# One scratch layout for the values of a neighbourhood attention: written column by column, without a second copy

## The chip, the cores and the metric

The kernel runs on one core of one Trainium2 chip, as one launch. The metric is the device time of that launch in microseconds (us). A core has five engines with an instruction queue each: TensorE (PE, with its weight loads shown apart as PEld), VectorE (DVE), ScalarE (ACT), GpSimd (POOL) and SyncE (SP). SP, ACT and POOL also issue DMA transfers, which sixteen DMA engines carry out. Each queue is worked off in order; between engines, semaphores order the work.

## The reference

One layer of a bidirectional encoder is computed for two sequences, a prompt of 1024 tokens and a sample of 512, with the same weights; model width 1024, head size 64, all in float32. Two token mixers work side by side: branch A is attention of 8 query heads over 2 key/value heads, branch B is attention over a neighbourhood of 8 rows × 16 columns on a grid that is 64 tokens wide (token t has row t // 64 and column t % 64).

```python
z = xn @ w_in            # q_A | k_A | v_A | q_B | k_B | v_B | gate_A | gate_B
o_a = _gqa_attention(qa, ka, va)
o_b = _neighbourhood_attention(qb, kb, vb, rpb)
merged = sigmoid(ga) * (o_a @ w_proj_a) + sigmoid(gb) * (o_b @ w_proj_b)
h = h + merged @ w_out
h = h + square(relu(rmsnorm(h) @ w_mlp_up)) @ w_mlp_down
```

A last RMSNorm follows. What matters here is v_B: 8 heads of 64 values for each token, projected token by token and later read as strips of the grid.

## The kernel before

Float32 products are made of three matmuls on a high and a low part of each operand (`mm3`); a value of branch B is therefore kept as 128 numbers, its 64 high parts and 64 low parts.

The kernel runs `run` for the sample first (called trunk 0 here, NB = 1, names with `s0`), then for the prompt (trunk 1, NB = 2, names with `s1`), and then one MLP for both. In `run`, two rounds g = 0 and 1 follow each other, one for each half of the heads. A round has a projection stage and an attention stage of branch A:

- Projection stage (pool `phR`). `load_a` and `load_v` load the weights by SP into raw buffers (`rawp`, three of them) and split them into high and low parts (L199 on ACT, L206 on DVE). For each tile `tt` of 128 tokens, that is two rows of the grid, PE makes `z`; `values(tt - 2)` makes the values of branch B for four heads into `zv` and splits them into `vt` (L648 on ACT, L649 on DVE), a tile of 128 tokens × 4 heads × 128 numbers with two buffers; ACT issues its store to the scratch `vd` in DRAM (L652), one tile late, through `pending` and `flush`. `heads_t` transposes queries and keys, and ACT copies them to `kT` and `qT` (L626, L628). At a stage's end the values and heads of the last two tiles come close together, with some matmuls of a gate (`fill.pull`) between.
- Attention stage (pool `phA`). `s_tile` makes a tile of scores into one of two PSUM buffers (`big`, L772 and L773), DVE takes the maximum, ACT the exponential into a tile `p` (L778), POOL scales it (L781); PE transposes `p` and multiplies it by the values of branch A (`pv`). Between them stand matmuls of the gate of branch A (`gate`, `fill`), whose results ACT stores to `zg` (L435). `phA` reuses the SBUF memory of `phR`; a tile of the one waits for the last access, a DMA's too, to the tile of the other that lay there.

In trunk 1 the attention stage also issues, on SP, two copies per unit (L808), 16 per round, 32 in all, from DRAM to DRAM: from the scratch `vd`, whose rows are tokens, to four scratches `vst[j]`, one for each strip of 32 columns, in the order that branch B reads.

Branch B follows (pool `phB`). `prep_v(h, j)` loads a strip of the values of head h: in trunk 1 with one load from `vst[j]` (L950), in trunk 0 with four loads from `vd`, one for each row a of four (L956 to L958). `v_unit` multiplies by it. Then come `phG`, which merges the branches, and the MLP.

The order of instructions on every engine is set by a planner of the framework, which goes by the order of the program, by the readiness of operands and buffers and by costs of its own; some instructions are held in program order by hand. The stores of ACT and the loads of SP share eight DMA semaphores, and a transfer can wait for the one before it on the same semaphore, whichever queue that was on.

Of the kernel before, what the change touches and what calls it, by code (L numbers as in the profile page):

```python
# [11 lines left out]
F32 = mybir.dt.float32  # L12
# [6 lines left out]
P = 128  # L19
# [3 lines left out]
GRID_W = 64  # L23
# [38 lines left out]
def encoder(ctx: ExitStack, tc: tile.TileContext, xs, outs, w):  # L62
    nc = tc.nc
    dram = ctx.enter_context(tc.tile_pool(name="dram", bufs=1, space=bass.MemoryType.DRAM))
# [28 lines left out]
    def mm(name):  # L93
        return pmm.tile([P, 512], F32, tag="mm", name=name)
# [175 lines left out]
    def flush():  # L270
        while pending:
            pending.pop(0)()
# [117 lines left out]
    class Trunk:  # L390
# [22 lines left out]
        def xh(self, tb, c):  # L413
            return self.xhl[tb][0][c // 4][:, c % 4, :]
# [4 lines left out]
    def run(tr, nxt, first):  # L419
        N, x, T, NT, NB = tr.N, tr.x, tr.T, tr.NT, tr.NB  # L420
        xh, xl = tr.xh, tr.xl
        rows = T // GRID_W
        halves = rows // 8

        vd = dram.tile([T, 8, P], F32, name=f"vd{N}")
        vst = [dram.tile([rows // 4, 32, 4, 8, P], F32, name=f"vst{N}_{j}") for j in range(4)] if NB == 2 else None
        zg = [dram.tile([D, T], F32, name=f"zg{N}_{i}") for i in range(2)]
        oad = dram.tile([4 * P, T], F32, name=f"oad{N}")
        obd = dram.tile([4 * P, T], F32, name=f"obd{N}")
# [99 lines left out]
        for g in range(2):  # L529
            with phase(f"phR{N}_{g}") as ph:  # L530
# [107 lines left out]
                def values(tt):  # L638

                    tb, j = divmod(tt, 4)  # L640
                    nm = f"{N}_{g}_{tt}"
                    js = slice(j * P, (j + 1) * P)
                    zv = mm(f"zv{nm}")[:, :256]
                    for k in range(NC8):
                        mm3(zv, xh(tb, k)[:, js], xl(tb, k)[:, js], wv[k][0], wv[k][1], k == 0, k == NC8 - 1)
                    vt = pre.pop("vt", None) or ph.tile([P, 4, P], F32R, tag="vt", name=f"vt{nm}", bufs=2)
                    zv4 = zv.rearrange("p (h d) -> p h d", d=HD)
                    nc.scalar.activation(vt[:, :, 0:HD], zv4, AF.Copy)  # L648
                    nc.vector.tensor_tensor(vt[:, :, HD:P], zv4, vt[:, :, 0:HD].bitcast(F32), op=ALU.subtract)  # L649
                    flush()  # L650
                    pending.append(
                        lambda: nc.scalar.dma_start(vd[tt * P : (tt + 1) * P, 4 * g : 4 * g + 4, :], vt.bitcast(F32))  # L652
                    )

                def chain(tt, z, rt):
# [34 lines left out]
                for tt in range(NT):  # L690
                    tb, j = divmod(tt, 4)
# [68 lines left out]
            with phase(f"phA{N}_{g}") as ph:  # L760
                units = [(h, qb) for h in range(4) for qb in range(NB)]
                PP = {}

                def s_tile(u, j):
                    h, qb = u
                    nm = f"{N}_{g}_{h}_{qb}_{j}"
                    q0 = (qb * 4 + j) * P
                    lhs = qT[h % 2][:, h // 2, q0 : q0 + P]
                    s = big(f"s{nm}")[:, :T]
                    for kb in range(NB):  # L770
                        ks = slice(kb * 512, kb * 512 + 512)
                        nc.tensor.matmul(s[:, ks], lhs, kT[:, 0, ks], start=True, stop=False)  # L772
                        nc.tensor.matmul(s[:, ks], lhs, kT[:, 1, ks], start=False, stop=True)  # L773
                    nm_ = sml.tile([P, 1], F32, tag="nm", name=f"nm{nm}")
                    nc.vector.tensor_reduce(nm_, s, axis=AX.X, op=ALU.max, negate=True)  # L775
                    p = ph.tile([P, T], F32, tag="P", name=f"p{nm}", bufs=8)
                    l = sml.tile([P, 1], F32, tag="l", name=f"l{nm}")
                    nc.scalar.activation(p, s, AF.Exp, bias=nm_, accum_out=l)  # L778
                    rl = sml.tile([P, 1], F32, tag="rl", name=f"rl{nm}")
                    nc.vector.reciprocal(rl, l)  # L780
                    nc.gpsimd.tensor_scalar(p, p, rl, 1.0, op0=ALU.mult, op1=ALU.mult)  # L781
                    PP[u, j] = p

                o_of = {}

                def pv(u, kc, hi, lo):
                    h, qb = u
                    if kc == 0:
                        o_of[u] = mm(f"o{N}_{g}_{h}_{qb}")
                    o = o_of[u]  # L790
                    nc.tensor.matmul(o, vhl[:, kc, :], hi, start=(kc == 0), stop=False)
                    nc.tensor.matmul(o, vhl[:, kc, :], lo, start=False, stop=(kc == NT - 1))
                    if kc == NT - 1:
                        r0 = (g * 4 + h) * HD
                        finish_o(o, 512, oad[r0 : r0 + HD, qb * 512 : qb * 512 + 512], ph, f"A{N}_{g}_{h}_{qb}")

                for j in range(4):
                    s_tile(units[0], j)
                    fill.pull(2)
                queue = []  # L800
                LAG = 2
                for ui, u in enumerate(units):
                    h, qb = u
                    if NB == 2:
                        hs = slice(4 * g, 4 * g + 4)
                        for a in range(2 * (ui % 2), 2 * (ui % 2) + 2):
                            c0 = (0, 8, 24, 32)[ui // 2]
                            nc.sync.dma_start(  # L808
                                vst[ui // 2][:, :, a, hs, :].rearrange("k c h d -> k c (h d)"),
                                vd[:, hs, :].rearrange("(k a c) h d -> a k c (h d)", a=4, c=GRID_W)[a, :, c0 : c0 + 32],  # L810
                            )
                    if first:
                        bias_row(g * 4 + ui)
                        if g == 0 and ui == 1:
                            early["a"] = load_a(1)
                        if g == 0 and ui == 2:
                            early["v"] = load_v(1, slot)
                    nxt_u = units[ui + 1] if ui + 1 < len(units) else None
                    sdone = 0
                    for kc in range(NT):  # L820
                        pt = mm(f"pT{N}_{g}_{h}_{qb}_{kc}")
                        for j in range(4):
                            nc.tensor.transpose(  # L823
                                pt[:, j * P : (j + 1) * P], PP[u, j][:, kc * P : (kc + 1) * P], ident
                            )
                        hi = ph.tile([P, 512], F32R, tag="pth", name=f"pth{N}_{g}_{h}_{qb}_{kc}", bufs=3)
                        lo = ph.tile([P, 512], F32R, tag="ptl", name=f"ptl{N}_{g}_{h}_{qb}_{kc}", bufs=3)
                        nc.scalar.activation(hi, pt, AF.Copy)  # L828
                        nc.vector.tensor_tensor(lo, pt, hi.bitcast(F32), op=ALU.subtract)  # L829
                        queue.append((u, kc, hi, lo))  # L830
                        if nxt_u is not None:
                            while sdone < 4 and kc >= ((0, 1, 3, 4) if NB == 2 else (0, 0, 1, 2))[sdone]:
                                s_tile(nxt_u, sdone)
                                sdone += 1

                        fill.pull(1 if NB == 1 or kc % 4 < 3 else 0)
                        if len(queue) > LAG:
                            pv(*queue.pop(0))
                fill.drain()
                for item in queue:  # L840
                    pv(*item)
# [80 lines left out]
        with phase(f"phB{N}") as ph:  # L922
# [22 lines left out]
            def prep_v(h, j):  # L945
                if h not in strips:
                    strips[h] = slot([P, 4, rows // 4, P], F32R, f"vs{N}_{h}")
                v = strips[h]
                if NB == 2:
                    nc.sync.dma_start(  # L950
                        v[:, j, :, :].bitcast(F32), vst[j][:, :, :, h, :].rearrange("k c a d -> (c a) k d")
                    )
                    return
                c0 = (0, 8, 24, 32)[j]
                for a in range(4):
                    nc.sync.dma_start(  # L956
                        v[a * 32 : a * 32 + 32, j, :, :].bitcast(F32),
                        vd[:, h, :].rearrange("(k a c) d -> a c k d", a=4, c=GRID_W)[a, c0 : c0 + 32],  # L958
                    )

            def load_qk(pr, hold=None):
# [229 lines left out]
            for i in range(n + 4 - NB):  # L1191
                if moved:
                    slot_no[0] = i
                if i < n - 8:
                    f = (5 if i < 2 else 2 + i % 2) if NB == 1 else 5 - (i % 6 == 5)
                else:
                    f = 3 + i % 2 if NB == 1 else 8
# [3 lines left out]
                if i < n:  # L1201
# [4 lines left out]
                    h, j = units[i]  # L1206
# [57 lines left out]
        with phase(f"phG{N}") as ph:  # L1264
# [65 lines left out]
            for half in range(2):  # L1330
                wo = wos[half]
                hc = slice(half * 512, half * 512 + 512)
                for tt in range(NT):
                    tb, j = divmod(tt, 4)
# [53 lines left out]
                    if half == 1:  # L1388
# [12 lines left out]
                        else:  # L1401
# [10 lines left out]
                            if 3 <= tt <= 5:  # L1412
                                j = tt - 3
# [563 lines left out]
```

## Time and profile before

| what | before |
|---|---|
| median of 3 runs | 2136.41 us (2136.06 to 2136.95) |
| the profiled execution | 2136.87 us, of which the span from first to last instruction is 2135.0 us |
| granted TensorE clock, mean | 0.997 of full speed |
| copies `vst <- vd` (L808) | 32 of 256 KB, on SP, issued from 452.2 to 791.2 us |
| stores `vd <- vt` (L652) | 24 of 256 KB, on ACT, issued from 35.1 to 652.7 us |
| strip loads `vs <- vst` (L950) | 32 of 256 KB, on SP |
| strip loads `vs <- vd` (L956) | 128 of 32 KB, on SP |

The page of the profile gives busy time by engine, the span in 40 slices with the granted clock and the DMA engines' mean busy share, the DMA queues, and the costliest groups of instructions. Further views are a list of waits (who waited for whom, total, times, longest), a timeline (start, duration, engine, line, operation, tiles; in brackets the idle time before it and what ended it; neighbours of one kind are merged, "x6"), and windows (for a stretch of time: its length, then the busy time and the count of instructions of PE, PEld, DVE, ACT and POOL, the granted clock, the share of the DMA engines and GB/s). A small q behind an engine's name (SPq, ACTq) is its queue of DMA issues; the duration there is that of issuing, not of the transfer. L212 and L206 are helpers that many stages use, so tiles tell stages apart: `zvs` is the value projection, `ss` the scores of branch A, `gpss` a gate.

### The profile page before, as it was taken

The page shows a single profiled execution, that of the slowest core. Times are in us where ns is not written, and L with a number is a line of the kernel's source. Part 1 is how long each engine was busy: PE and PEld are TensorE (multiplying, and loading weights), DVE is VectorE, ACT ScalarE, POOL GpSimd, SP SyncE. Part 2 cuts the span into 40 slices and gives each one's busy share as a digit, 9 for nine tenths or more (in the row PEclk, how much of TensorE's full clock was granted, in tenths as well). Part 3 has the DMA queues.
Part 4 walks back from the last instruction along what each step waited for, and adds up shares of the span by engine and source line. Part 5 has one row for each costly group of instructions (what it writes and reads, how often), then busy time and mean ns, then how long its engine had stood idle before and what let it go on. Part 6 is the DMA issues. An engine that isn't in the chain of part 4 may idle for free.

```text
span 2135.0 us, 31762 instructions
## 1 busy us (share of the span) xinstructions
PE 2099.9 (98%) x10871; PEld 1840.2 (86%) x10871; DVE 1483.2 (69%) x2793; ACT 1146.3 (54%) x2487; POOL 362.0 (17%) x446
## 2 busy tenths in 40 slices
PE   9999999999989999999999999999999999999998
PEld 8888778988888888888888899999999988888887
DVE  6665786767647756787882877778777777759563
ACT  6664653767556645555531556556655643434352
POOL 2232310323233314442101200003000000000000
PEclk9999999999999999999999999999999999999999
DMA  6437557520133038876472666578445799688561
GB/s 192 133 99 212 148 165 254 184 89 29 59 111 107 25 97 245 244 219 196 153 246 103 203 196 193 162 249 210 158 146 158 259 351 344 215 276 282 166 203 64
DMA packets 340072, 381.31 MB, mean 179 GB/s; under 512 B 30911, under 2 KB 267079, under 8 KB 339911
## 3 DMA queue, kind: packets, MB, share of 16 engines
q1 hardware_dynamic: 301687, 313.99, 46.9%
q10 hardware_dynamic: 31072, 45.11, 6.0%
q0 software_dynamic: 7152, 20.19, 3.5%
q8 instruction: 86, 1.41, 0.3%
q14 instruction: 75, 0.61, 0.1%
HBM read 282.68 MB, written 105.71 MB: 182 GB/s over the span
## 4 chain that ended last, share of the span: by engine, by line
PE 53%; DVE 1%; issue 0%; ACT 0%; POOLq 0%; POOL 0%; ACTq 0%; DVEq 0%
PE dn L212 20%; PE ua L212 6%; PE ud L212 6%; PE uc L212 6%; PE ops L212 4%; PE ub L212 3%; PE ppbs L212 2%; PE ppas L212 2%; PE dnf L212 2%; PE pt L353 0%; PE obs L212 0%; PE gpss L212 0%; PE sbs L212 0%; PE ptbs L1126 0%; DVE A L1452 0%
## 5 line engine op out<-in xcount | busy, mean ns | idle before, releaser
L212 PE MATMUL dn<-wd,ah 128*128 128x512 f32 x1248 | 384.3, 389 | 0.0
L212 PEld LDWEIGHTS dn<-wd,ah 128*128 128x128 f32 x1248 | 234.2, 188 | 48.7
L212 PE MATMUL dn<-wd,al 128*128 128x512 f32 x624 | 242.8, 389 | 0.0
L1451 ACT ACTIVATE ah<-ar 128x512 fp32r<-128x512 f32 x168 | 104.4, 628 | 206.0 <-PE dn L212 186.7
L212 PE MATMUL gpss<-xs_0h,w_gs 128*128 128x512 f32 x512 | 188.7, 402 | 0.8 <-DVE ot_Bs L472 0.4
L1452 DVE TENSOR_TENSOR al<-ar,ah 128x512 fp32r<-128x512 f32 x168 | 114.4, 687 | 75.5 <-ACT ah L1451 67.9
L212 PE MATMUL ud<-B,A 128*128 128x384 f32 x768 | 143.6, 334 | 0.7 <-DVE c L1569 0.7
L212 PE MATMUL uc<-B,A 128*128 128x384 f32 x768 | 143.7, 334 | 0.0
L212 PE MATMUL ua<-B,A 128*128 128x384 f32 x768 | 138.8, 334 | 0.0
L212 PEld LDWEIGHTS dn<-wd,al 128*128 128x128 f32 x624 | 117.1, 188 | 24.2
L781 POOL TENSOR_SCALAR ps<-ps,rls 128x1024 f32<-128x1024 f32 (+1 forms) x96 | 96.8, 1010 | 226.4 <-DVE rls L780 201.0
L212 PEld LDWEIGHTS ud<-B,A 128*128 128x128 f32 x768 | 133.9, 188 | 1.1 <-DVE c L1569 1.1
L212 PEld LDWEIGHTS uc<-B,A 128*128 128x128 f32 x768 | 134.1, 188 | 0.2 <-ACT A L1451 0.2
L212 PEld LDWEIGHTS ua<-B,A 128*128 128x128 f32 x768 | 133.7, 188 | 0.2
L829 DVE TENSOR_TENSOR ptls<-pTs,pths 128x512 fp32r<-128x512 f32 x160 | 107.7, 686 | 37.3 <-ACT pths L828 36.3
L828 ACT ACTIVATE pths<-pTs 128x512 fp32r<-128x512 f32 x160 | 94.0, 597 | 73.4 <-PE pTs L823 71.3
L212 PE MATMUL ops<-wh_os,mgs 128*128 128x512 f32 x384 | 119.4, 390 | 0.0
L775 DVE TENSOR_REDUCE nms<-ss 128x1 f32<-128x1024 f32 (+1 forms) x96 | 99.9, 1041 | 25.6 <-PE ss L773 25.1
L212 PEld LDWEIGHTS gpss<-xs_0h,w_gs 128*128 128x128 f32 x512 | 96.3, 189 | 18.9 <-DVE w_gs L206 0.7
L778 ACT ACTIVATE ps<-ss,nms 128x1024 f32<-128x1024 f32 (+1 forms) x96 | 93.2, 972 | 23.4 <-DVE nms L775 20.6
L180 POOL TENSOR_TENSOR rs_f<-ms_f,mhalf 128x1 f32<-128x1 f32 x6 | 4.0, 667 | 590.7 <-DVE ms_f L176 590.7
L823 PEld LDWEIGHTS pTs<-ident,ps 128*128 128x128 f32 x640 | 77.7, 140 | 28.6 <-POOL ps L781 4.3
(287 smaller groups left out, 5152.4 us busy)
## 6 DMA issues: line engine op xcount, KB each, us to landing
ar<-ud SPq DMA_DIRECT2D x120, 512.0 KB
br<-in_w_mlp_down_dram SPq DMA_DIRECT2D x72, 512.0 KB
rawu<-in_w_mlp_up_dram SPq DMA_DIRECT2D x64, 512.0 KB
ud<-c ACTq DMA_DIRECT2D x128, 192.0 KB
raw_gs<-in_w_in_dram SPq DMA_DIRECT2D x32, 512.0 KB
ud<-cs SPq DMA_DIRECT2D x64, 192.0 KB
tbs<-pbs SPq DMA_DIRECT2D x24, 384.0 KB
bhs<-tbs SPq DMA_DIRECT2D x24, 384.0 KB
```

The source lines that it names most:

```text
L180: nc.gpsimd.tensor_tensor(r[:, :n], m[:, :n], mhalf[:, :n], op=ALU.pow)
L212: op = nc.tensor.matmul(out, a, b, **kw)
L775: nc.vector.tensor_reduce(nm_, s, axis=AX.X, op=ALU.max, negate=True)
L778: nc.scalar.activation(p, s, AF.Exp, bias=nm_, accum_out=l)
L781: nc.gpsimd.tensor_scalar(p, p, rl, 1.0, op0=ALU.mult, op1=ALU.mult)
L823: nc.tensor.transpose(pt[:, j * P : (j + 1) * P], PP[u, j][:, kc * P : (kc + 1) * P], ident)
L828: nc.scalar.activation(hi, pt, AF.Copy)
L829: nc.vector.tensor_tensor(lo, pt, hi.bitcast(F32), op=ALU.subtract)
L1451: nc.scalar.activation(hi, src, AF.Copy)
L1452: nc.vector.tensor_tensor(lo, src, hi.bitcast(F32), op=ALU.subtract)
```

## The change

The scratch `vd` gets a layout of its own: group of four rows, column, row in the group, head, numbers. The four scratches `vst` and the copies into them go. The store of a value tile writes its two rows of 64 tokens side by side into each column, so its destination counts 2 rows × 64 columns × 2 KB, where its source still counts 128 partitions × 2 KB. A strip of trunk 1 is loaded from `vd` itself, with one load; the loads of trunk 0 read the same bytes from the new places. What is computed stays the same.

```diff
-        vd = dram.tile([T, 8, P], F32, name=f"vd{N}")
-        vst = [dram.tile([rows // 4, 32, 4, 8, P], F32, name=f"vst{N}_{j}") for j in range(4)] if NB == 2 else None
+        vd = dram.tile([rows // 4, GRID_W, 4, 8, P], F32, name=f"vd{N}")
...
                     flush()
+                    to = vd[tt // 2, :, tt % 2 * 2 : tt % 2 * 2 + 2, 4 * g : 4 * g + 4, :]
                     pending.append(
-                        lambda: nc.scalar.dma_start(vd[tt * P : (tt + 1) * P, 4 * g : 4 * g + 4, :], vt.bitcast(F32))
+                        lambda: nc.scalar.dma_start(
+                            to.rearrange("c r h d -> r c (h d)"), vt.bitcast(F32).rearrange("p h d -> p (h d)")
+                        )
                     )
...
-                    if NB == 2:
-                        hs = slice(4 * g, 4 * g + 4)
-                        for a in range(2 * (ui % 2), 2 * (ui % 2) + 2):
-                            c0 = (0, 8, 24, 32)[ui // 2]
-                            nc.sync.dma_start(
-                                vst[ui // 2][:, :, a, hs, :].rearrange("k c h d -> k c (h d)"),
-                                vd[:, hs, :].rearrange("(k a c) h d -> a k c (h d)", a=4, c=GRID_W)[a, :, c0 : c0 + 32],
-                            )
...
+                c0 = (0, 8, 24, 32)[j]
                 if NB == 2:
                     nc.sync.dma_start(
-                        v[:, j, :, :].bitcast(F32), vst[j][:, :, :, h, :].rearrange("k c a d -> (c a) k d")
+                        v[:, j, :, :].bitcast(F32), vd[:, c0 : c0 + 32, :, h, :].rearrange("k c a d -> (c a) k d")
                     )
                     return
-                c0 = (0, 8, 24, 32)[j]
                 for a in range(4):
                     nc.sync.dma_start(
                         v[a * 32 : a * 32 + 32, j, :, :].bitcast(F32),
-                        vd[:, h, :].rearrange("(k a c) d -> a c k d", a=4, c=GRID_W)[a, c0 : c0 + 32],
+                        vd[:, c0 : c0 + 32, a, h, :].rearrange("k c d -> c k d"),
                     )
```

## The prediction

> **What bounds the kernel now.** I read the page's span and busy rows first, then PE's own waits, then the timeline around the longest of them. "Trunk 0" is the sample (512 tokens, first), "trunk 1" the prompt (1024).
>
> ```profile
> span 2135.0 us, 31762 instructions
> PE 2099.9 (98%) x10871; PEld 1840.2 (86%) x10871; DVE 1483.2 (69%) x2793; ACT 1146.3 (54%) x2487; POOL 362.0 (17%) x446
> PE zvs L212 <- ACT wh_vs L199: 5.7, 1, 5.7
> PE sbs L212 <- DVE kBs L1015: 2.3, 2, 1.8
> ```
>
> TensorE is the bound: it idles about 35 us of 2135. So nothing is won by lighter transfers as such; a change counts only where PE waits, or comes to wait. PE's longest wait by far is a single one of 5.7 us on L199, the split of the value weights (`load_v`). Its chain, from the timelines of SP, ACT and PE:
>
> ```profile
> 538.33 0.41 DVE L206 TENSOR_TENSOR wgls<-rawkvs,wghs 128x256 fp32r<-128x256 f32 x1
> 574.53 12.34 SPq L808 DMA_DIRECT2D vsts<-vds  x6
> 586.99 4.00 SPq L245 DMA_DIRECT2D raw_vs<-in_w_in_dram  x2
> 598.32 1.06 ACT L199 ACTIVATE wh_vs<-raw_vs 128x1024 fp32r<-128x1024 f32 x1 [3.29 <-DMA raw_vs<-in_w_in_dram]
> 599.43 0.58 PE L212 MATMUL zvs<-wh_vs,xs_0h 128*128 128x256 f32 x1 [5.74 <-ACT wh_vs L199]
> 599.40:605.60 6.20, 5.59 (x24) 5.00 (x24) 0.00 (x0) 0.00 (x0) 0.53 0.27 77
> 436.70:439.66 2.96, 2.88 (x25) 2.69 (x23) 0.00 (x0) 0.00 (x0) 1.00 0.26 94
> ```
>
> SP issues in order. Six of the copies that the change removes (L808) stand ahead of the two loads of the value weights of trunk 1's second half; these go out at 586.99, share the engines with copies still moving, and PE stands until 599.43. The last two rows are windows of tile zvs alone: its 24 matmuls then take about 6.2 us at a granted clock of 0.53, where 25 took 2.96 us at 1.00, so 24 take 2.8 to 2.9. The stall costs 5.74 plus 6.17 − 2.88 = 3.29: **9.0 us** in all.
>
> **The change, part by part.** *Removed:* 32 copies `vst <- vd`.
>
> ```profile
> L808 SPq DMA_DIRECT2D vsts<-vds x32: 579/580/1127, 452.2 to 791.2; - x32
> L652 ACTq DMA_DIRECT2D vds<-vts x24: 326/326/368, 35.1 to 652.7; - x24
> SPq L808 <- DMA oads<-os_As: 29.7, 5, 9.3
> ```
>
> SP loses 32 issues of 0.58 us and the waits before them (the third row is the one that holds the last ones). The raw buffers that the load fills come free long before 587 (the last split that reads one ends at 538.7, first row of the chain above), so the load goes out early, or, if the planner leaves it at 587, meets empty queues: 1 MB at the 317 GB/s of the write below is 3.3 us, with the start and a split of 1.06 some 6, hence before 593.7, where PE came to stand. Either way the stall goes: −9.0. What is late next there is nothing that I see; bounds 0 and −9.0, and I take −9.0, the measured stall. Behind the 16 copies of trunk 1's second half (up to 791) the one longer wait in PE's list, sbs with 1.8, comes 190 us later; 0.
>
> *Reads (L950, L958):* as many pieces of 512 B, at other strides. They go out a head or several units ahead of the matmuls that use them, and none of PE's waits names them: 0, and without that cover a load's few us, once.
>
> *Writes (L652):* this is where the price is. The tile's 128 rows of 2 KB used to go to 128 evenly spaced rows. Now row and column swap: the destination is 2 × 64 pieces, outermost count 2. Windows in which only one such transfer moves show what an outermost count does:
>
> ```profile
> 437.52 0.33 ACTq L652 DMA_DIRECT2D vds<-vts  x1
> 438.36:439.18 0.82, 0.82 (x9) 0.82 (x8) 0.27 (x1) 0.82 (x3) 0.00 (x0) 1.00 0.84 317
> 531.05:534.55 3.50, 3.50 (x21) 2.97 (x20) 3.36 (x6) 2.72 (x5) 1.12 (x1) 1.00 0.23 74
> 562.42:565.74 3.32, 3.32 (x21) 2.75 (x20) 2.43 (x5) 2.50 (x6) 1.13 (x1) 1.00 0.24 78
> ```
>
> Both move 256 KB (0.82 us at 317 GB/s; 3.50 at 74). The write, 128 rows on both sides, has 0.84 of the 16 DMA engines busy; the copy, whose source is 4 × 32 rows, 0.23 to 0.24, four engines. I read this as: the outermost count is what gets spread. An outermost 2 then leaves two engines. Work per transfer: 0.82 × 0.84 × 16 = 11.0 engine-us for the write, 3.50 × 0.23 × 16 = 12.9 for the copy; on two engines **5.5 to 6.4 us** in place of 0.8. I take 5.5, its own row. It starts about 1.0 us after issue (437.52 to 438.36, rounded up).
>
> [...]
>
> Mid-stage this is hidden: `vt` has two buffers, and a write has about a tile's period to land (7 us, 437.52 to 444.42, two neighbouring writes). At the four ends of the projection stages the last tiles crowd, and I follow the last three writes A, B, C. The last tile's `vt` (L648, on ACT, ahead of the kT copies) needs A; then the exponentials L778 put their results where the pool before held `vt`, and need B and C. Trunk 1, first half, then second:
>
> ```profile
> 444.42 0.33 ACTq L652 DMA_DIRECT2D vds<-vts  x1
> 449.27 0.33 ACTq L652 DMA_DIRECT2D vds<-vts  x1
> 449.69 0.38 ACT L648 ACTIVATE vts<-zvs 128x256 fp32r<-128x256 f32 x1
> 451.27 0.33 ACTq L652 DMA_DIRECT2D vds<-vts  x1
> 455.86 1.12 ACT L778 ACTIVATE ps<-ss,nms 128x1024 f32<-128x1024 f32 x1 [0.48 <-DVE nms L775]
> 457.33 0.39 PE L772 MATMUL ss<-kTs,qTs 128*128 128x512 f32 x1
> 645.65 0.34 ACTq L652 DMA_DIRECT2D vds<-vts  x1
> 651.79 0.39 ACT L648 ACTIVATE vts<-zvs 128x256 fp32r<-128x256 f32 x1 [1.05 <-DMA vds<-vts]
> 658.26 1.12 ACT L778 ACTIVATE ps<-ss,nms 128x1024 f32<-128x1024 f32 x1
> 660.45 0.39 PE L772 MATMUL ss<-kTs,qTs 128*128 128x512 f32 x1
> ```
>
> First half: A moves 445.4 to 450.9, so the last `vt` starts 1.2 late and C is issued at 452.5. B ends at 456.4, C at 461.9. The exponential waits from 455.86 to 461.9, +6.0. PE's third score tile needs the score bank that it frees (at 455.86 + 1.12 = 456.98) and started at 457.33, 0.35 later: PE stands 5.7 us. At 6.4 us a write: A 451.8, B 458.2, C 464.6, stall 8.4. Behind the exponential ACT's whole queue stands, and PE's own order is fixed, so the gate matmuls behind that score tile can't fill in.
>
> Second half, same steps: the row at 651.79 shows that this wait exists already. A 646.7 to 652.2, B 657.7, C 663.2; the second exponential +4.9, PE's slack 660.45 − (658.26 + 1.12) = 1.07, stall 3.9 (6.4 a write: 6.6). Trunk 0, second half and first:
>
> ```profile
> 121.69 0.33 ACTq L652 DMA_DIRECT2D vds<-vts  x1
> 126.45 0.35 ACTq L652 DMA_DIRECT2D vds<-vts  x1
> 128.46 0.36 ACTq L652 DMA_DIRECT2D vds<-vts  x1
> 132.67 0.68 ACT L778 ACTIVATE ps<-ss,nms 128x512 f32<-128x512 f32 x1
> 134.44 0.39 PE L772 MATMUL ss<-kTs,qTs 128*128 128x512 f32 x1
> 44.42 0.33 ACTq L652 DMA_DIRECT2D vds<-vts  x1
> 49.13 0.38 ACT L648 ACTIVATE vts<-zvs 128x256 fp32r<-128x256 f32 x1
> 50.80 0.28 ACT L626 ACTIVATE kTs<-pqs 128x128 fp32r<-128x128 f32 x1 [1.28 <-PE pqs L622]
> ```
>
> Second: A 122.7 to 128.2, B 133.7, C 139.2; exponential +6.5, slack 134.44 − (132.67 + 0.68) = 1.09, stall 5.4 (8.1). First: only A matters (that stage's pool begins with the inputs, so `vt` lies elsewhere): 45.4 to 50.9, the last `vt` +1.8, kT and PE behind it about 1.6 (2.5).
>
> Stalls: 5.7 + 3.9 + 5.4 + 1.6 = **16.6 us** (high end 8.4 + 6.6 + 8.1 + 2.5 = 25.6). Each longer stall may also cost clock, as the one at 599 did (3.3 after 5.74). A shorter one did too:
>
> ```profile
> 987.41 1.28 PE L212 MATMUL sbs<-kBs,qBs 128*128 128x384 f32 x3 [1.84 <-DVE kBs L1015]
> 987.40:991.00 3.60, 3.58 (x10) 3.07 (x11) 3.51 (x9) 2.55 (x5) 0.79 (x2) 0.53 0.31 91
> ```
>
> 1.84 us of idling, then 3.6 us at 0.53, some 1.7 lost. For the three stalls I take 3.3 + 3.3 + 1.7 = 8.3, bounds 0 and 9.9. [...]
>
> The write's issue on ACT may grow from 0.33 to the copy's 0.58, 24 × 0.25 = 6 us of an engine busy 54%: 0 to 1 on PE, taken as 0.
>
> **Sum.** +16.6 + 8.3 − 9.0 = +15.9. The profiled run took 2136.87 (span 2135.0 and 1.9 around it): 2152.8. The runs' median lies 0.5 lower, 2136.41, so **2152.3**. The case's own range: 16.6 + 0 − 9.0 = +7.6 to 25.6 + 9.9 − 9.0 = +26.5, 2144 to 2163.
>
> **Rivals.**
> - *The write keeps its engines* (faster). If it is spread over four engines or more, 11.0 / 4 = 2.75 us each, C would land at about 455.2, before the exponential at 455.86: nothing is late, and only the −9.0 is left: 2127.4. For it: the source still has 128 rows, and the trace shows no transfer with 128 on the SBUF side and 2 on the other. Against it: the copies had 128 evenly spaced rows on one side too (their destination), and got four.
> - *Two engines, but the value weights still come late* (slower still), because the planner puts their load behind another store in SP's queue, as it put the copies behind `oads`: the −9.0 falls away, 2161.3. Against it: the raw buffers are free by 538.
> - *Two engines, and the ends absorb it*: the planner orders gate matmuls ahead of the score tile, or A, B, C overlap better than one behind the other; half of the stalls and little clock, 8 to 9 us, cancels the gain: 2136 ± 4.
>
> **How the numbers follow.** About 0.2% (4.3 us) is what a measurement of this kernel tells from no change. Forecast 0.55, late weights 0.15, absorbed 0.10, full width 0.20. Slower 0.70, same 0.10, faster 0.20. The range takes in the full-width case at its foot, and of the late-weights case the middle: 2126 to 2166.
>
> **What would show it.** Right: a window on one L652 write alone with a DMA share near 0.12; L778 and L648 waiting on vds at 50, 130, 452 and 655; PE waits "ss <- ACT" of 4 to 6 us there, with clock dips; no zvs wait near 594. Wrong: a share near 0.8 for that write, or PE's waits for ss unchanged; or zvs still waiting for wh_vs.

## The result: 2167.5 us, slower by 1.46%

The kernel after takes 2167.49 us (median of 4 runs, 2167.30 to 2169.47), before, beside it, 2136.68: ratio 1.0146, 95% interval 1.0128 to 1.0163. That is 30.8 us more where 15.9 were forecast, and 1.5 us above the range. The profiled run's span is 2165.2 us, 30.2 more than before.

Span and busy rows of the kernel after:

```profile
span 2165.2 us, 31728 instructions
PE 2108.4 (97%) x10871; PEld 1847.1 (85%) x10871; DVE 1481.3 (68%) x2793; ACT 1146.1 (53%) x2487; POOL 364.1 (17%) x446
```

PE's longest waits in it (total, times, longest):

```profile
PE ss L774 <- ACT kTs L625: 20.2, 4, 7.1
PE ss L774 <- ACT ps L780: 11.2, 5, 4.5
PE sbs L212 <- DVE kBs L1009: 2.3, 2, 1.8
```

Before, the longest wait of the scores `ss` was this:

```profile
PE ss L772 <- ACT kTs L626: 2.1, 2, 1.2
```

PE is busy 8.5 us longer with as many instructions (2108.4 against 2099.9), because the granted clock falls at the stalls: in the window from 51 to 71 us it is 0.74 on average, where it was 1.00 before the change. The remaining 21.7 us are idle time. The wait of `zvs` is gone; two waits of the scores `ss` have come or grown, on the kT copies (L625) and on the exponentials (L780). Where they lie, from PE's timeline (in brackets the idle time before a matmul), with the ends of trunk 0's rounds 0 and 1, then trunk 1's:

```profile
59.15 0.79 PE L774 MATMUL ss<-kTs,qTs 128*128 128x512 f32 x1 [7.06 <-ACT kTs L625]
...
142.43 0.50 PE L774 MATMUL ss<-kTs,qTs 128*128 128x512 f32 x1 [3.98 <-ACT kTs L625]
...
152.12 0.50 PE L774 MATMUL ss<-kTs,qTs 128*128 128x512 f32 x1 [2.78 <-ACT ps L780]
...
475.25 0.79 PE L774 MATMUL ss<-kTs,qTs 128*128 128x512 f32 x1 [3.81 <-ACT kTs L625]
...
485.95 0.50 PE L774 MATMUL ss<-kTs,qTs 128*128 128x512 f32 x1 [3.19 <-ACT ps L780]
...
678.97 0.79 PE L774 MATMUL ss<-kTs,qTs 128*128 128x512 f32 x1 [5.31 <-ACT kTs L625]
...
691.70 0.79 PE L774 MATMUL ss<-kTs,qTs 128*128 128x512 f32 x1 [4.52 <-ACT ps L780]
```

All are at the four stage ends. What they wait for, from ACT's timeline, at each end: the issue of write A (the third to last of the stage, as in the prediction), then the last `vt`, which waits for it.

```profile
45.28 0.51 ACTq L652 DMA_DIRECT2D vds<-vts  x1
...
57.40 0.38 ACT L647 ACTIVATE vts<-zvs 128x256 fp32r<-128x256 f32 x1 [7.26 <-DMA vds<-vts]
...
132.17 0.53 ACTq L652 DMA_DIRECT2D vds<-vts  x1
...
140.69 0.38 ACT L647 ACTIVATE vts<-zvs 128x256 fp32r<-128x256 f32 x1 [3.43 <-DMA vds<-vts]
...
463.40 0.50 ACTq L652 DMA_DIRECT2D vds<-vts  x1
...
472.86 0.38 ACT L647 ACTIVATE vts<-zvs 128x256 fp32r<-128x256 f32 x1 [3.46 <-DMA vds<-vts]
...
666.52 0.50 ACTq L652 DMA_DIRECT2D vds<-vts  x1
...
677.22 0.38 ACT L647 ACTIVATE vts<-zvs 128x256 fp32r<-128x256 f32 x1 [5.60 <-DMA vds<-vts]
```

From A's issue to that `vt` pass 12.1, 8.5, 9.5 and 10.7 us; the prediction had 6.5 everywhere. The next fence has windows on the DMA engines (the last two numbers are their busy share and GB/s). The first is a write alone in the middle of a stage. The next two are trunk 0's first end, from A's issue to its first packet (48.5; a write has 128 packets of 2 KB), and the last stretch before A landed. The last two are trunk 1's second end, from A's issue to its first packet (670.1), and from there to its landing.

```profile
653.50:659.50 6.00, 6.00 (x42) 6.00 (x41) 2.11 (x6) 2.75 (x16) 2.30 (x3) 1.00 0.13 42
...
45.30:48.50 3.20, 3.20 (x23) 2.94 (x22) 3.11 (x7) 2.57 (x11) 0.00 (x0) 1.00 0.67 195
...
54.00:56.80 2.80, 0.00 (x0) 0.00 (x0) 0.00 (x0) 0.00 (x0) 0.00 (x0) 0.56 0.13 50
...
666.50:670.00 3.50, 3.50 (x25) 3.21 (x25) 2.63 (x6) 1.16 (x5) 1.25 (x2) 1.00 0.89 259
670.00:676.70 6.70, 3.66 (x17) 2.53 (x15) 1.56 (x4) 1.58 (x6) 0.00 (x0) 0.91 0.55 169
```

Alone, a write has 0.13 of 16 engines, two, for some 6.2 us (issued at 652.25, packets from 653.4 to 659.6). At the ends SP's loads move beside it, and A's first packet comes 1.6 to 3.6 us after the issue instead of 1.1. At trunk 1's second end the write ahead of A was also still moving, until 667.2. In the stretch from 54.0 the share is 0.13 again, yet packets of A and of the load `rawqs` both move, about 8 of each in half a microsecond, where the next write, alone from 58.0 on, moves 12 or 13 (over the whole of a lone write it is 10 on average, 128 in 6.2 us). A share of 0.13 is two engines, so both move on these two: there they take turns, while the load's part on the other 14 is done (its landing is recorded in sixteen parts, fourteen from 51.5 to 53.1, the last two at 58.1 and 58.2).

### The profile page after: what moved, and what is told of

The parts are those of the page before. It is cut to its first block, busy times and chain, and to the rows that moved or that the text cites. A ratio compares the mean times of both kernels' runs of the same rounds, so it can differ in the third digit from the quotient of the medians.

```text
span 2165.2 us, 31728 instructions
## 1 busy us (share of the span) xinstructions
PE 2108.4 (97%) x10871; PEld 1847.1 (85%) x10871; DVE 1481.3 (68%) x2793; ACT 1146.1 (53%) x2487; POOL 364.1 (17%) x446
## 3 DMA queue, kind: packets, MB, share of 16 engines
q10 hardware_dynamic: 30736, 45.11, 6.0%
## 4 chain that ended last, share of the span: by engine, by line
PE 51%; DVE 1%; issue 0%; ACT 0%; POOLq 0%; POOL 0%; ACTq 0%; DVEq 0%
PE dn L212 19%; PE ua L212 6%; PE ud L212 6%; PE uc L212 6%; PE ops L212 4%; PE ub L212 3%; PE ppbs L212 2%; PE ppas L212 2%; PE dnf L212 2%; PE pt L353 0%; PE obs L212 0%; PE ptbs L1120 0%; PE sbs L212 0%; DVE A L1446 0%; ACT pbs L1076 0%
## 5 line engine op out<-in xcount | busy, mean ns | idle before, releaser
L212 PEld LDWEIGHTS dn<-wd,ah 128*128 128x128 f32 x1248 | 234.2, 188 | 48.5
L780 ACT ACTIVATE ps<-ss,nms 128x1024 f32<-128x1024 f32 (+1 forms) x96 | 93.2, 972 | 39.1 <-DVE nms L777 19.9
L774 PE MATMUL ss<-kTs,qTs 128*128 128x512 f32 x160 | 71.7, 448 | 32.8 <-ACT kTs L625 20.2
```

The source lines that it names most:

```text
L212: op = nc.tensor.matmul(out, a, b, **kw)
```

## The experiments

Theory: the outermost count of 2 keeps a write on two engines; at the stage ends it lands late, the later because SP's loads share those engines; the removal of the copies is worth the 9 us forecast. The rivals are in each expectation. Times are medians, with the ratio to before; the spread of a kernel's runs is 2 to 6 us.

| kernel | us | ratio, 95% interval |
|---|---|---|
| oldplain: row by row, no copies | 2128.19 | 0.9959 (0.9946 to 0.9973) |
| oldpad4: the same, outermost count 4 | 2142.45 | 1.0028 (1.0018 to 1.0038) |
| oldpad2: the same, outermost count 2 | 2168.38 | 1.0148 (1.0135 to 1.0162) |
| rows16: after, two stores a tile | 2135.82 | 0.9995 (0.9986 to 1.0004) |
| rowspin: rows16, pairs kept together | 2129.82 | 0.9967 (0.9954 to 0.9979) |
| ends_only: rowspin at the last three tiles alone | 2136.84 | 1.0001 (0.9992 to 1.0010) |
| vt_memory: after, other memory for `vt` | 2151.68 | 1.0071 (1.0057 to 1.0084) |
| more_loads: after, more transfers at two ends | 2182.04 | 1.0213 (1.0199 to 1.0227) |
| loads_held: after, loads held at two ends | 2163.93 | 1.0129 (1.0113 to 1.0144) |
| interleave: oldplain, other partitions | 2127.31 | 0.9957 (0.9945 to 0.9970) |

### The removal alone (oldplain) and the outermost count (oldpad2, oldpad4)

The kernel before without the copies, `vd` row by row; trunk 1 takes the four loads of trunk 0's form. These loads put a strip's keys in another order than the probabilities have, so trunk 1's branch B sums other products; instructions and bytes are as they would be.

```diff
-                        for a in range(2 * (ui % 2), 2 * (ui % 2) + 2):
-                            nc.sync.dma_start(vst[ui // 2]..., vd...)
...
-                if NB == 2:
-                    nc.sync.dma_start(v[:, j, :, :]..., vst[j]...)
-                    return
```

> The kernel before with its copies left out and its row-by-row layout kept; trunk 1 loads each strip straight from the scratch in four loads, as trunk 0 does. It is the removal alone. Theory: the wait of zvs goes and nothing is late, about 2127.5 us (9.0 less than before). Rival (removing the copies costs, or four loads for a strip are late in branch B): 2137 us or more.

Then the unused column behind each row of 64 (oldpad2, shown here against oldplain) or each run of 32 (oldpad4); the loads' addresses follow:

```diff
-        vd = dram.tile([T, 8, P], F32, name=f"vd{N}")
+        vd = dram.tile([T // 64, 65, 8, P], F32, name=f"vd{N}")
...
-                        lambda: nc.scalar.dma_start(vd[tt * P : (tt + 1) * P, 4 * g : 4 * g + 4, :], vt.bitcast(F32))
+                            vd[2 * tt : 2 * tt + 2, 0:64, 4 * g : 4 * g + 4, :].rearrange("r c h d -> r c (h d)"),
+                            vt.bitcast(F32).rearrange("p h d -> p (h d)"),
```

> The kernel of the run without copies, row by row, with one unused column behind each grid row (65 instead of 64), so that a store's two rows can't be one run and its outermost count is 2; the columns are not turned. Theory (the count 2 decides): two engines, gaps as in the kernel after, about 2167 us. Rival (turning the columns decides): about 2127.5 us.

> As the run with the unused column, but with it behind every 32 columns (33 for 32), so that the outermost count of a store is 4. Strips 1 and 2 of branch B are loaded from the columns of strips 0 and 3, in the same number of loads and bytes, so the values that they multiply are others. The prediction's bound (with four engines nothing is late): 3 us for a store, about 2127.5 us. Theory with sharing (SP's loads on the same engines lengthen write A where they meet it, at the ends of trunk 0's round 0 and trunk 1's round 1): a few us of gaps are left there, 2129 to 2136 us.

oldplain takes 8.1 us less than before, and `zvs` no longer waits. oldpad2 takes 2168.38, as the kernel after, with its columns not turned and its waits nearly the same; so the outermost count does it, and neither the turned columns nor the single load of a strip. Its PE waits:

```profile
PE ss L774 <- ACT kTs L625: 20.0, 4, 6.8
```

Outermost 4 takes 14.3 us more than the 128 rows of oldplain, against 40.2 for outermost 2. The bound of the prediction, nothing late from four engines on, falls, and the theory with sharing (2129 to 2136 us) was short as well. A write of oldpad4 alone in the middle of a stage:

```profile
629.00:633.00 4.00, 4.00 (x29) 4.00 (x28) 1.14 (x4) 1.51 (x12) 2.30 (x3) 1.00 0.25 66
```

0.25 is four engines; the write, issued at 627.63, landed by 633.0, 5.4 us later where 3.75 were reckoned (1.0 + 2.75). The packets agree with the shares: a write before the change (0.84) ends with sixteen packets of 4 bytes, a copy (0.23) with four, a write of the kernel after (0.13) with two. ACT's queue moves 45.11 MB in all these runs, and its packets differ by just that for 24 writes: 31072 packets in oldplain, 336 fewer in oldpad2 (30736, as in the kernel after), 288 fewer in oldpad4 (30784).

### All engines in the new layout (rows16, rowspin), and at the ends alone (ends_only)

```diff
+                    def write():
+                        for r in range(2):
+                            nc.scalar.dma_start(
+                                to[:, r].rearrange("c h d -> c (h d)"),
+                                vt[64 * r : 64 * r + 64].bitcast(F32).rearrange("p h d -> p (h d)"),
+                            )
```

> The kernel after, with each store of values issued as two, one for each grid row of the tile (64 partitions, destination 64 x 512 elements), so that the outermost count of the destination is 64 and no longer 2; the layout and the loads stay. Theory (the outermost count of 2 keeps a store on two DMA engines, it lands late at the four stage ends, and without that only the gain of 9.0 from the copies that went is left): the store's DMA share is about 1.0, the gaps of PE on the kTs copies and on exp go, about 2128 us; one more issue for each store on ACT may cost up to 1. Rival (columns 16 KB apart are slow to write in themselves, whatever the engines): still about 2167 us. Rival (the order of the work without the copies costs): between, 2137 or more.

2135.82: 31.7 us of the lateness go, yet not all; the time lies between the theory's and the rivals'. ACT's queue has 31456 packets, 720 more than in the kernel after: sixteen at the end of each of 48 stores in place of two at each of 24, so a store is on 16 engines. A pair is two issues. In ACT's timeline at trunk 1's second end they stand apart:

```profile
650.16 0.45 ACTq L654 DMA_DIRECT2D vds<-vts  x1
653.15 0.39 ACT L647 ACTIVATE vts<-zvs 128x256 fp32r<-128x256 f32 x1 [2.66 <-DMA vds<-vts]
653.17 1.95 ACTq L654 DMA_DIRECT2D vds<-vts  x3
```

The planner had put the second half of a pair behind the next `vt`, which itself waits. But PE's largest gap in rows16 is at trunk 1's first end, where the pairs stand together; there ACT waits 2.66 us for A and then 2.15 for the load `rawkvs`, ahead of the kT copy:

```profile
458.70 0.80 PE L778 MATMUL ss<-kTs,qTs 128*128 128x512 f32 x1 [4.23 <-ACT kTs L625]
```

rowspin pins the two halves of each pair (`keep_in_program_order`):

> The kernel after with two stores for each tile (16 engines each), as the first run, but the two are kept next to each other on ACT's queue; in the first run the second of a pair was issued up to 3 us behind the first, behind a wait of the next vt. Theory (the order on ACT kept the first run from the 2128 of the kernel without copies): 2128 to 2131 us. Rival (two issues for each tile, or the columns' layout at 16 engines, cost the 7.6 us): 2135 to 2137 us.

2129.82, within the first theory's numbers. The rest was thus the order that pinning changes, though not only the split pair shown above, and writing in columns costs little or nothing on 16 engines (oldplain, row by row, took 2128.19). ends_only keeps pairs for A, B and C and one store on two engines for the other tiles:

```diff
+                    if tt < NT - 3:
+                        pending.append(lambda: nc.scalar.dma_start(to..., vt...))
+                        return
```

> The kernel after with pairs of stores (16 engines each, next to each other on ACT's queue) for the last three tiles of each projection stage alone; the other tiles keep one store on two engines. Theory (only writes A, B and C matter, the others are hidden by the tiles' period): as with pairs everywhere, 2129.8 us, or up to 1 less for the issues saved. Rival (the writes in the middle cost too, or the one ahead of A delays it): 2133 us or more.

2136.84; the rival's number. Trunk 1's second end, PE, then ACT, then a window from A's issue on:

```profile
653.77 0.78 PE L787 MATMUL ss<-kTs,qTs 128*128 128x512 f32 x1 [3.94 <-ACT kTs L625]
```

```profile
652.21 0.38 ACT L647 ACTIVATE vts<-zvs 128x256 fp32r<-128x256 f32 x1 [4.42 <-DMA vds<-vts]
```

```profile
646.00:651.80 5.80, 3.83 (x18) 2.69 (x16) 1.56 (x4) 1.76 (x7) 0.00 (x0) 1.00 0.89 273
```

A, on 16 engines (ACT's queue has 31096 packets, 360 more than in the kernel after, for 24 half stores with sixteen and 12 stores with two) and issued by 646.1, lands at 651.8: SP's loads keep the engines 0.89 busy. So of the 37.7 us between after and rowspin, 30.7 belong to the last three tiles and 7.0 come with the writes of the middle. PE is busy as long in both (2099.9 and 2099.6 us), so the difference is idle time. How the writes of the middle reach the ends (the write ahead of A, or loads that they hold up) isn't settled. The order changes with them too: at this end rowspin issues A at 641.64, 3.9 us behind the last of SP's loads, ends_only beside it (645.57 and 645.59). That only A, B and C matter is refuted; that the middle's writes cost by landing late is not shown.

### What waits (vt_memory)

```diff
-                    vt = pre.pop("vt", None) or ph.tile([P, 4, P], F32R, tag="vt", name=f"vt{nm}", bufs=2)
+                    vt = pre.pop("vt", None) or (vtp if NB == 1 and g else ph).tile(
+                        [P, 4, P], F32R, tag="vt", name=f"vt{nm}", bufs=4 if g else 2
+                    )
...
```

> The kernel after, stores on two engines as they are. Trunk 0's round 1: vt gets four buffers in memory of its own that the attention stage doesn't reuse. Trunk 1's round 1: four buffers in the stage's pool, which the attention stage does reuse. Rounds 0 as before. Theory (a late landing costs only by what waits for the memory): at trunk 0's round 1 both gaps of PE go (3.98 and 2.78, back to about 1.2), though the stores land as late as before; at trunk 1's round 1 the gap on kTs (5.31) goes and the one on exp (4.52) grows to 8 to 10, since write C lands no sooner; rounds 0 keep 7.06 and 3.81 + 3.19. Together 8 to 10 less than after: about 2158 us. Rival (the wait of the last vt is a cost of its own, behind which write C is issued late): the exp gap of trunk 1's round 1 stays near 4.5: about 2152 us.

PE at trunk 0's second end and at trunk 1's:

```profile
138.38 0.50 PE L779 MATMUL ss<-kTs,qTs 128*128 128x512 f32 x1 [1.36 <-ACT kTs L628]
...
672.72 0.50 PE L779 MATMUL ss<-kTs,qTs 128*128 128x512 f32 x1 [2.60 <-ACT ps L785]
```

At trunk 0's the two gaps are 1.36 in all, as before the change (1.22 there), with writes B and C landing only at about 144.7 and 150. So a late landing costs nothing there by itself; what costs is the memory that it keeps. At trunk 1's the gap on kTs is down to 0.61, but the one on exp is 2.60, neither the 8 to 10 of the theory nor 4.5. ACT's timeline has another cause for it:

```profile
668.01 3.40 ACTq L434 DMA_DIRECT2D zgs<-sgs  x1
671.46 1.11 ACT L785 ACTIVATE ps<-ss,nms 128x1024 f32<-128x1024 f32 x1 [3.48 <-issue]
```

The first exponential stood behind the issue of the gate's store, which took 3.40 us here and 0.32 in the kernel after; what held that issue isn't shown. The rival's total of 2152 thus came true for another reason than its own. Nor did C hold the second exponential: C landed at 681, after that exponential had begun (674.79, right behind B's landing at 674.4). So with four buffers it can't lie over C's buffer. Which write an exponential waits for is a matter of where the pool puts tiles.

### The loads beside the writes (more_loads, loads_held)

```diff
+                    if tt == NT - 3 and (NB, g) in ((1, 1), (2, 0)):
+                        for i in range(4):
+                            extra = dram.tile([P, 4, P], F32, name=f"extra{N}_{g}_{i}")
+                            nc.sync.dma_start(extra, vt.bitcast(F32))
```

> The kernel after with four additional transfers of 256 KB on 16 engines (0.8 us each), asked for by SP when write A's source is ready, at the ends of trunk 0's round 1 and trunk 1's round 0 alone; their results are not used. Theory (other transfers on the two engines lengthen write A): the gaps on kTs there grow from 3.98 and 3.81 by about 3 us each, and those at the other two ends (7.06, 5.31) stay: 2173 to 2178 us. Rival (A's time is only that of its own bytes on two engines): the gaps stay, 2167 to 2169 us.

Write A's landing moved as the theory has it. After its issue it took 8.04 us at trunk 0's second end in the kernel after and now 11.27; at trunk 1's first, 9.07 and now 12.24. But the gaps on kTs grew by 12.1 and 10.7, not by 3, while those on exp there went, and 2182.04 is above the theory's 2173 to 2178. At trunk 1's first end ACT's timeline shows the rest:

```profile
482.67 0.38 ACT L647 ACTIVATE vts<-zvs 128x256 fp32r<-128x256 f32 x1 [6.54 <-DMA vds<-vts]
483.55 0.50 ACTq L656 DMA_DIRECT2D vds<-vts  x1
491.85 0.63 ACT L199 ACTIVATE wghs<-rawkvs 128x512 fp32r<-128x512 f32 x1 [8.79 <-DMA rawkvs<-in_w_in_dram]
492.39 0.26 ACT L625 ACTIVATE kTs<-pqs 128x128 fp32r<-128x128 f32 x1
```

The last `vt` is 3.1 later (6.54 for 3.46), and then ACT waits 8.79 us for a load of SP's, ahead of the kT copy on ACT's queue (1.16 in the kernel after). So with the added transfers the load came late as well as the write. That it took turns with the writes on the two engines, as a load did at 54.0 us in the kernel after, is not shown here. At trunk 0's end `vt` itself stood 14.5 us, 8 of them after A had landed. What it waited for there is write B, which landed at 150.3, just ahead of `vt` at 150.38. Why it needs B in this kernel isn't known, so this end says nothing beyond A's landing.

loads_held goes the other way; a POOL instruction on one column of the target makes the loads wait:

```diff
+                if late is not None:
+                    nc.gpsimd.tensor_tensor(raw[:, 0:1], late, late, op=ALU.mult)
...
+                    if h == 0:
+                        nc.gpsimd.tensor_tensor(v[:, j, 0, 0:1], mark, mark, op=ALU.mult)
```

> The kernel after, stores on two engines, but two groups of SP's loads are held until the attention stage has its first probabilities (a POOL instruction on one column writes into their target before): the query and key weights at the end of trunk 0's round 0, and branch B's first four strips (1 MB) at the end of trunk 1's round 1. Theory (loads that share the two engines made write A land later there than the prediction's 6.5 us after issue): A lands 1 to 2 us sooner at the first and 2 to 3.5 sooner at the second, the gaps on kTs fall from 7.06 to 5 to 6 and from 5.31 to 2 to 3.5; in all 3 to 8 less than after, 2160 to 2165 us. Rival (the two engines' own 6.2 us and what waits for it explain all, the loads nothing): gaps unchanged, 2167 us.

PE at trunk 0's first end and trunk 1's second:

```profile
57.30 0.79 PE L779 MATMUL ss<-kTs,qTs 128*128 128x512 f32 x1 [6.07 <-ACT kTs L630]
...
677.35 0.79 PE L779 MATMUL ss<-kTs,qTs 128*128 128x512 f32 x1 [4.59 <-ACT kTs L630]
...
688.19 0.50 PE L779 MATMUL ss<-kTs,qTs 128*128 128x512 f32 x1 [1.49 <-ACT ps L785]
```

The time fell by 3.6 to 2163.93, inside the theory's 2160 to 2165. Term by term it is weaker: A lands 1.0 sooner after its issue at both ends (1 to 2 and 2 to 3.5 were expected), the kTs gaps fall by 1.0 and 0.7, and most comes from exp at trunk 1's end (4.52 to 1.49). The loads of branch B's query and key weights and of a gate stayed, the key weights going out 4.7 us sooner.

### A faster kernel (interleave)

The difference to oldplain is the partitions that the four loads of a strip go to:

```diff
-                        v[a * 32 : a * 32 + 32, j, :, :].bitcast(F32),
+                    to = v[a * 32 : a * 32 + 32] if NB == 1 else v[a : P : 4]
...
+                        to[:, j, :, :].bitcast(F32),
```

> The kernel before without its copies, row-by-row layout, stores on 16 engines; trunk 1's strip is loaded from the scratch in four loads, each to every fourth partition (the order of the keys that the weights have), where the earlier run put it to 32 neighbouring partitions. Theory (only the removal counts, the loads are hidden): as the earlier run without copies, 2128 us, faster than both kernels. Rival (loads to every fourth partition are slower and come late in branch B): 2130 us or more, with PE waits for vss.

2127.31, 0.43% faster than before. Its busy row and PE's longest waits; no `vs` is among them:

```profile
PE 2096.9 (99%) x10871; PEld 1839.0 (87%) x10871; DVE 1480.8 (70%) x2793; ACT 1147.3 (54%) x2487; POOL 360.7 (17%) x446
```

```profile
PE ss L771 <- ACT kTs L625: 2.5, 3, 1.2
PE sbs L212 <- DVE kBs L1002: 2.3, 2, 1.8
```

## Why the prediction was right in direction and short in size

Against interleave, which has the removal and nothing late, the kernel after's span is 39.8 us longer: 11.5 of PE's busy time (2108.4 − 2096.9) and 28.3 of idling. The prediction had 8.3 and 16.6.

- **The removal, −9.0**: right. 8.1 less in oldplain, 9.1 in interleave.
- **Two engines from the outermost count**: right, by oldpad2 and by the share of 0.13. The rival in which the write keeps its engines falls. So does the one with late value weights, since no wait for `wh_vs` is left, and so does the one in which the ends absorb the lateness, since 29.4 us of idling came there.
- **"5.5 to 6.4 us in place of 0.8"**, "about 1.0 us after issue": right for a write alone (6.2 and 1.1), though the 5.5 that was taken is 0.7 short.
- **The step that failed** is the carrying of these two numbers to the stage ends ("A moves 445.4 to 450.9", and alike at the others). There SP's loads move too, and A took 8.5 to 12.1 us from issue to the `vt` that waits, not 6.5. In idle time of PE, net of what was idle there before:

| end | forecast | measured |
|---|---|---|
| trunk 0, round 0 | 1.6 | 7.1 |
| trunk 0, round 1 | 5.4 | 5.5 |
| trunk 1, round 0 | 5.7 | 6.9 |
| trunk 1, round 1 | 3.9 | 9.8 |
| together | 16.6 | 29.4 |

  The two ends with the smallest forecast are those where A took longest. more_loads shows that transfers beside it lengthen A (+3.2 twice), loads_held that taking some away shortens it (−1.0 twice). At the first end A's first packet came 2.1 us later after the issue than that of a write alone, and its packets then took 8.5 us in place of 6.2; this was read from the packets and not tried.
- **The waiters**: the memory chain (`vt` needs A, exp needs the memory) was right, by vt_memory at trunk 0's second end. But the prediction laid the stalls of trunk 0's round 1 and trunk 1's round 0 on exp alone; 3.98 and 3.81 of them came already on the kT copies behind the last `vt`, whose delay it had put at 1.2 in trunk 1 and passed over in trunk 0.
- **Clock, 8.3 (0 to 9.9)**: 11.5, over the upper bound. There are seven gaps of 2.7 us or more where three stalls had been counted. Behind six of them the granted clock is 0.50 for 3 to 10 us. Behind the gap of 3.19 at 485.95 it stays at 1.00 (486 to 496 us), where before the change one of 1.84 had been enough, so the length of a gap alone doesn't give its price.
- **"Mid-stage this is hidden"**: not borne out. With the middle's writes left on two engines the kernel takes 7.0 us more (ends_only against rowspin), by a way that is open.
- **Four engines suffice**: wrong, by 14.3 us (oldpad4). A write took 5.4 us from issue to landing there, not 3.75.
- **The reads, 0**: no PE wait names them. Yet where they move they matter: holding 1 MB of them back was part of the 3.6 that loads_held gained.
- **The issue on ACT**: 0.50 us for 0.33, and nothing on PE names it.

## What to carry to other kernels

Before a copy is turned, look at the outermost count of each side: it, and not the bytes, set the time of these writes (256 KB in 0.8 us with 0.84 of the engines busy, in 6.2 with 0.13), and a store split by rows, or the plain layout with four small loads, gave the same gain without the price. The time of a write alone was too short for the stage ends, where the next stage's loads move too (8.5 to 12.1 us in place of 6.5): add what else is in flight before working out who is late. And a late landing cost by the memory that it held (5.5 us of idling at trunk 0's second end, 0.1 with memory of its own), so look which instruction reuses it.

## Not expected of the hardware

- A load and a write that shared two engines took turns (about 8 packets each in half a microsecond, where the next write alone moved 12 or 13), so the load, spread over 16 engines, ended as late as its part on the slow two (58.2 us, 53.1 on the others): at 54.0 to 56.8 us the share was 0.13 with both under way.
- Two issues were themselves long while such writes were under way. SP's issue of a gate's weights at trunk 1's second end took 5.55 us, 0.69 before the change, and the gate's store on ACT in vt_memory 3.40 for 0.32. What holds an issue was not tried.

```profile
669.41 5.55 SPq L245 DMA_DIRECT2D raw_gs<-in_w_in_dram  x1
```

- A late write also held up a load, by way of ACT and VectorE. The second load `rawqs` of trunk 0's first end went out at 58.91 us, 50.95 before the change. Its issue took 0.37 in both; it waited for the split of a gate's weights on VectorE (L206), which stood behind the last `vt`.
- On four engines a write took 5.4 us from issue to landing, where a fourth of the full-width write's engine time, and 1.0 to the start, gave 3.75.
- Where the strips of trunk 1 come in 16 small loads (interleave), SP needs 12.07 us to issue them, and the window from A's issue to the last `vt` has a share of 0.50; with four loads (ends_only) it was 0.89. That the spacing helps was only read, not tried.
